# Delta rule: both directions of a chunk through the inverse in one tile, and the chunk's front joined likewise

## The chip, the cores and the metric

The kernel runs on 1 core of one Trainium2 chip. The metric is the device time of one execution in microseconds (us). TensorE multiplies matrices, VectorE, ScalarE and GpSimd work on tiles in SBUF (VectorE and ScalarE also read TensorE's results from PSUM), SyncE (SP) issues most transfers.

## What is computed

One layer of a hybrid encoder for 1024 tokens of width 1024 with 16 meta tokens ahead. Half of the mixer is a gated delta rule with 4 heads of 128, run forward and backward over the sequence; the other half is attention with 8 query heads. Both are projected out together, and a squared-ReLU MLP follows. The delta rule, in chunks, is what the change touches:

```python
decay = exp(where(incl, gc[..., :, None] - gc[..., None, :], -inf))
kk = einsum('bnhik,bnhjk->bnhij', k, k)
a_low = where(strict, kk * decay * beta[..., :, None], 0.0)
rhs = concatenate([v * beta[..., None], k * (beta * exp(gc))[..., None]], axis=-1)
uw = lax.linalg.triangular_solve(a_low + eye(C), rhs, left_side=True, lower=True, unit_diagonal=True)
...
def step(S, xs):
    v_new = u_i - w_i @ S
    o_i = q_i @ S + qk_i @ v_new
    S = S * gl_i + k_i.T @ v_new
```

## The kernel before

The kernel uses chunks of 128 tokens, so 8 per direction, and replaces the triangular solve by an explicit inverse of the unit triangular matrix of each chunk, head and direction (lower for the forward direction "f", upper for the backward one "b"). It is one program in which about twenty Python generators ("streams") each write out their own work in small steps. `progress` (L1538) decides the order in which the steps are written: it holds a clock of matmul time by its own formula (L88), a step that yields is due again after the latency in `LAT` (L79; 1.5 us for the inverse), and of the streams that are due the first in `URGENCY` (L74) goes next. The inverse stands ahead of the projection GEMM in that list, so its steps go in between the GEMM's groups of matmuls. The order of execution can still differ from the order in which steps are written, as the framework that builds the program places each engine's instructions.

The order of the stages: projection GEMM (`gemm`, L667), with short convolutions and norms behind each piece; beside it, as soon as keys and gates are there, `front` (L955), `kq_stream` (L1001) and the inverse; then `chain_open` (L1036) and the chain over the chunks (`chain`, L1065), which runs beside attention; the output projection; the MLP.

- `consts` (L32) makes the constant matrices on the host; `cgroup` (L142) loads a group of them in pieces of 512 columns through two staging tiles, `kdf` and `kdb`, and casts each on VectorE (L150).
- `open_prep` (L746) loads two such groups, the second (`dmg`, L760) with 14 masks of 128 columns and two of 128 for the decay, 2048 columns in all, and fills the fixed columns of the PM tiles with `pm_rest` (L777) on GpSimd.
- `front(c)`: the products of the keys (kk), the decays of both directions (exp on ScalarE, L970), their product dn (L972), the unit diagonal put in on GpSimd (L809), which gives the fp16 high part ah, and the low part al on VectorE (L978). Then the scaled keys kd (L988) and their store. It waits for the inverse and kq of chunk c - 2.
- `invert` (L820) for one direction of one chunk with 4 heads, in 15 steps. A first step transposes ah into X and masks X and Y (L833, L834). Then six levels of two steps: 4 matmuls of 64 columns into one PSUM tile and a mask on VectorE into pm (L844); 8 matmuls into one PSUM tile and two copies on ScalarE, into X and Y (L854, L855), with `pm_rest` on GpSimd. Then a correction step (9 matmuls, L865) and the result tt (4 matmuls, L870).
- Four streams run it, `inv00`, `inv10`, `inv01` and `inv11` (direction, parity of the chunk). The last one first inverts the meta tokens' matrix (`meta_inverse`, L895), with one head and three levels.
- `kq_stream`: products of keys and queries times the decay (L1016), stored.
- PSUM: psa has 3 tiles of 512 columns that the inverse, front and kq share (`psr`, L115); psg has 5 for the GEMM.
- `q_stream` (L1182) opens attention after the GEMM and the chain's opening.

Of the kernel before, what the change touches and what calls it, by code (L numbers as in the profile page):

```python
# [73 lines left out]
URGENCY = ("consts", "meta", "inv00", "inv10", "inv01", "inv11", "front", "kq", "chn", "chain0", "chain1", "wout", "wload",  # L74
# [7 lines left out]
def body(tc, I, out, dbg=None):  # L82
# [397 lines left out]
    def gates():  # L480
        for e in range(8):
            S.dma_start(ba[e * NM:(e + 1) * NM, :, 64:65], msscr[:, 0:16].rearrange("p (s e) -> p s e", s=2)[:, :, e:e + 1])
        tmp_g = keep("Df", 512)
# [262 lines left out]
    def open_prep():  # L746
# [4 lines left out]
        def stage():  # L751
            turn.append(0)
            return keep("kd" + "fb"[len(turn) % 2], 512)
# [6 lines left out]
        dmg = cgroup("f1", "ngt", F16, np_, stage)  # L760
# [7 lines left out]
        R.update(mk=mk, blk=blk, dm={(s, b): dmg(f"{s}{b}") for s in "fb" for b in (1, 2, 4, 8, 16, 32, 64)}, id16=id16, out=[dmg("nlt"), dmg("ngt")])  # L768
        for side in ("f0", "b0", "f1", "b1"):
            for i in range(2):  # L770
                PM[side, i] = np_.tile([P, NH * P], F16, name=f"pm{side}{i}", bufs=1)
                pm_rest(PM[side, i], NH, 2 << i, side[0] != "b")
            yield
# [3 lines left out]
    def pm_rest(pm, nh, b, lower):  # L777

        G.tensor_scalar(cols(pm, b, not lower).rearrange("p (h n) c -> p h n c", h=nh), rep4(cols(idf, b, not lower), nh),
                        1.0, 1.0, ALU.mult, ALU.mult)  # L780

    def rep4(ap, nh):
        return ap.unsqueeze(1).broadcast_to([P, nh, ap.shape[1], ap.shape[2]])
# [36 lines left out]
    def invert(nh, ah, al, side, key, levels, tt):  # L820

        w = nh * P
        lower = side == "f"
        other = "b" if lower else "f"
        dm, id16 = R["dm"], R["id16"]
        xy = keep("xy" + key, 2 * NH * P, F16)
        X, Y = xy[:, :w], xy[:, w:2 * w]
        ps = psr()  # L830
        for h in range(nh):
            T.matmul(v3(ps)[:, h], lhsT=v3(ah)[:, h], rhs=id16, start=True, stop=True)
        V.tensor_tensor(v3(X), v3(ps[:, :w]), rep(dm[side, 1], nh), ALU.mult)  # L833
        V.tensor_tensor(v3(Y), v3(ah), rep(dm[other, 1], nh), ALU.mult)  # L834
        yield
        for i, b in enumerate(levels):
            pm = PM[key, i % 2][:, :w]
            nb = 64 // b
            ps = psr()
            pv = ps[:, :w // 2].rearrange("p (h n c) -> p h n c", h=nh, c=b)  # L840
            for h in range(nh):
                T.matmul(pv[:, h], lhsT=v3(ah)[:, h], rhs=cols(v3(X)[:, h], b, lower), start=True, stop=True)
            mask = cols(dm[side, b], b, lower)
            V.tensor_tensor(cols(pm, b, lower).rearrange("p (h n) c -> p h n c", h=nh), pv,  # L844
                            rep4(mask, nh), ALU.mult)
            yield
            ps = psr()
            px = ps[:, :w // 2].rearrange("p (h n c) -> p h n c", h=nh, c=b)
            py = ps[:, w // 2:w].rearrange("p (h n c) -> p h n c", h=nh, c=b)
            for h in range(nh):  # L850
                T.matmul(px[:, h], lhsT=v3(Y)[:, h], rhs=cols(v3(pm)[:, h], b, lower), start=True, stop=True)
            for h in range(nh):
                T.matmul(py[:, h], lhsT=v3(pm)[:, h], rhs=cols(v3(Y)[:, h], b, not lower), start=True, stop=True)
            A.copy(cols(X, b, lower), px.rearrange("p h n c -> p (h n) c"))  # L854
            A.copy(cols(Y, b, not lower), py.rearrange("p h n c -> p (h n) c"))  # L855
            if i + 2 < len(levels) or i % 2:
                pm_rest(pm, nh, levels[i + 2] if i + 2 < len(levels) else levels[1], lower)
            yield
        ps = psr()
        T.matmul(v3(ps[:, :w]), lhsT=id16, rhs=rep(id16, nh), start=True, stop=False)  # L860
        for h in range(nh):
            T.matmul(v3(ps)[:, h], lhsT=v3(ah)[:, h], rhs=v3(X)[:, h], start=False, stop=False)
            T.matmul(v3(ps)[:, h], lhsT=v3(al)[:, h], rhs=v3(X)[:, h], start=False, stop=h == nh - 1)
        gt = PM[key, 0][:, :w]
        V.tensor_tensor(gt, ps[:, :w], X, ALU.subtract)  # L865
        yield
        ps = psr()
        for h in range(nh):
            T.matmul(v3(ps)[:, h], lhsT=v3(gt)[:, h], rhs=v3(Y)[:, h], start=True, stop=True)
        V.tensor_tensor(tt, ps[:, :w], Y, ALU.add)  # L870
        pm_rest(gt, nh, levels[0], lower)
# [11 lines left out]
    def consts_stream():  # L883
        yield from need("x")
        yield from open_prep()
        pl = keep("kdf", 512)
# [8 lines left out]
    def meta_inverse():  # L895
# [26 lines left out]
        yield from invert(1, ah, al, "f", "f1", (2, 4, 8), dn)  # L922
# [32 lines left out]
    def front(c):  # L955

        if c > 1:
            yield from need(f"inv0{c - 2}", f"inv1{c - 2}", f"kq{c - 2}")
# [3 lines left out]
        D, dn = {}, {}  # L962
        for d, side in FB:
            dn[d], D[d] = keep("dn" + side, 512), keep(f"D{side}{c % 2}", 512)
# [22 lines left out]
        for d, side in FB:  # L987
            V.tensor_tensor(v3(keep("kd" + side, 512)), v3(kT), bc(Erem[:, d, c], P), ALU.mult)  # L988
        yield
        for d, side in FB:  # L990
            S.dma_start(kscr[d * NT + c], keep("kd" + side, 512))
# [9 lines left out]
    def kq_stream():  # L1001

        yield from need("minv", *(f"q{h}" for h in range(NH)))
        for c in range(NT):
            yield from need(f"front{c}")
            D = {d: keep(f"D{side}{c % 2}", 512) for d, side in FB}
            qc = keep("qc", 512)
            S.dma_start(v3(qc), qscr[:, :, c * P:(c + 1) * P].rearrange("h p t -> p h t"))
            for d, side in FB:
                unit_diagonal(D[d], D[d])  # L1010
# [4 lines left out]
            for d, side in FB:  # L1015
                V.tensor_tensor(D[d], kq, D[d], ALU.mult)  # L1016
            yield
            for d, side in FB:
                S.dma_start(dscr[d * NT + c], D[d])
# [3 lines left out]
    def inv_stream(d, p):  # L1023

        side, key = "fb"[d], f"{'fb'[d]}{p}"
        if key == "f1":
            yield from meta_inverse()
        for c in range(p, NT, 2):
            yield from need(f"front{c}")
            tt = keep("tt" + side, 512)  # L1030
            yield from invert(NH, keep("ah" + key, 512, F16), keep("al" + key, 512, F16), side, key, (2, 4, 8, 16, 32, 64), tt)
            S.dma_start(tscr[d * NT + c], tt)
            mark(f"inv{d}{c}")


    def chain_open():  # L1036
        yield from need(*(f"inv{d}{c}" for d in range(2) for c in (NT - 2, NT - 1)), "meta", "kq")
# [519 lines left out]
    streams = dict(consts=consts_stream(), meta=meta_stream(), **{f"inv{d}{p}": inv_stream(d, p) for p in range(2) for d in range(2)},  # L1557
# [333 lines left out]
```

## Time and profile before

| | us |
|---|---|
| median of 3 runs (lowest to highest) | 1415.5 (1413.3 to 1420.03) |
| profiled execution | 1416.07 |
| its span | 1414.2 |
| TensorE busy | 1342.7 (95%) |
| VectorE busy | 1029.3 (73%) |
| ScalarE busy | 835.5 (59%) |
| GpSimd busy | 295.4 (21%) |

A profile is one execution of the program. Its page gives busy times of the engines, the windows view the same for a stretch of time with the granted clock of TensorE (1.00 is 2.4 GHz), the waits view the idle times of an engine by what ended them, the lines view groups of instructions with their mean duration, the tile view the same for one tile with first and last start, and the timeline the instructions one after another. A busy TensorE is one with a matmul in flight, and as matmuls overlap, the pace shows in the starts and not in the busy time.

### The profile page before, as it was taken

Reading aid. Unit: us, or ns where it says so; the run is one execution under the profiler, and the core shown is the slowest. Engines: PE = TensorE matmul, PEld = TensorE weight load, DVE = VectorE, ACT = ScalarE, POOL = GpSimd, SP = SyncE. Lnnn points to the kernel's source line nnn. Section 1 sums busy time; section 2 is a strip of 40 time slices with the busy share of each in tenths; the row PEclk is TensorE's granted clock in tenths of the full one; section 3 lists DMA queues with packets and bytes.
Section 4 is the critical chain, followed back from the end, with each engine's and each line's share of the span. In section 5 each row is a group of like instructions: output and inputs, shape, how many; then the busy total and the mean of one; then the engine's idle time right before and its main releaser. Section 6 shows DMA issues by size and latency. Waiting matters only on the chain. (4 is left out here: it accounts for less than half of the span.)

```text
span 1414.2 us, 26476 instructions
## 1 busy us (share of the span) xinstructions
PE 1342.7 (95%) x9627; PEld 1027.1 (73%) x9627; DVE 1029.3 (73%) x1962; ACT 835.5 (59%) x1747; POOL 295.4 (21%) x386
## 2 busy tenths in 40 slices
PE   6999999999998998899998799999999999999996
PEld 6999888777998877677777444444444888888875
DVE  5636779788768979877765987777775588675675
ACT  6556565756546777866644676666665455445552
POOL 1210234343534456533321200000000000000000
PEclk9999999999998999889999799999999999999998
DMA  6312234344379999997994354444443984466341
GB/s 209 87 57 62 83 98 158 112 149 153 121 253 282 245 264 239 221 242 186 224 225 135 102 175 158 153 155 150 158 155 114 331 271 127 142 193 194 98 150 66
DMA packets 273355, 236.86 MB, mean 167 GB/s; under 512 B 147484, under 2 KB 201656, under 8 KB 273224
## 3 DMA queue, kind: packets, MB, share of 16 engines
q1 hardware_dynamic: 270056, 225.73, 55.3%
q10 hardware_dynamic: 3168, 9.44, 1.8%
q8 instruction: 76, 1.25, 0.4%
q14 instruction: 55, 0.45, 0.1%
HBM read 132.27 MB, written 69.28 MB: 143 GB/s over the span
## 5 line engine op out<-in xcount | busy, mean ns | idle before, releaser
L95 PEld LDWEIGHTS <-wh 128*128 128x128 f16 x896 | 88.1, 99 | 102.7 <-issue 1.9
L95 PE MATMUL a<-woah 128*128 128x512 f32 x672 | 158.6, 390 | 1.3 <-DVE woah L1734 1.2
L95 PE MATMUL a<-woal 128*128 128x512 f32 x672 | 157.4, 389 | 0.0
L95 PEld LDWEIGHTS a<-woah 128*128 128x128 f32 x672 | 125.9, 188 | 29.0 <-DVE woah L1734 2.0
L95 PEld LDWEIGHTS a<-woal 128*128 128x128 f32 x672 | 126.1, 188 | 26.2
L95 PE MATMUL a<-uh,wh 128*128 128x344 f32 (+2 forms) x340 | 122.3, 360 | 0.7 <-ACT cw L665 0.5
L1270 POOL TENSOR_TENSOR P<-t,P 128x640 f16<-128x640 f32 x64 | 99.4, 1555 | 106.8 <-ACT P L1268 85.0
L95 PE MATMUL a<-ul,wh 128*128 128x344 f32 (+2 forms) x340 | 118.7, 349 | 0.5 <-DVE ul L262 0.5
L95 PE MATMUL a<-uh,wl 128*128 128x344 f32 (+2 forms) x340 | 118.3, 348 | 0.0
L161 POOL TENSOR_TENSOR rs<-ms,mhalf 128x1 f32<-128x1 f32 (+1 forms) x33 | 19.1, 578 | 424.0 <-DVE rs L1797 304.6
L1254 DVE TENSOR_REDUCE mx<-S 128x1 f32<-128x1024 f32 x64 | 77.9, 1219 | 24.3 <-PE S L95 24.1
L1262 ACT ACTIVATE t<-S,nb 128x1024 f32<-128x1024 f32 x64 | 71.5, 1117 | 40.8 <-DVE nb L1255 29.2
L95 PEld LDWEIGHTS <-pT 128*128 128x128 f16 x1536 | 59.5, 100 | 42.0 <-issue 26.6
L95 PE MATMUL o<-VP,pT 128*128 128x65 f16 (+1 forms) x1536 | 73.6, 198 | 11.3 <-DMA pT<-P 9.8
L95 PEld LDWEIGHTS <-wl 128*128 128x128 f16 x448 | 43.9, 98 | 54.1 <-issue 1.7
L1731 ACT ACTIVATE woah<-fr,isf 128x512 fp32r<-128x512 f32 x54 | 39.2, 725 | 70.3 <-PE a L95 61.0
L1731 ACT ACTIVATE woal<-fr,isf 128x512 fp32r<-128x512 f32 x54 | 39.2, 726 | 68.4 <-PE a L95 66.2
L1268 ACT CAST P<-t 128x1024 f16<-128x1024 f32 x64 | 66.8, 1043 | 4.7 <-DVE t L269 1.8
L1733 DVE SCALAR_TENSOR_TENSOR woah<-fr,isf,woah 128x512 fp32r<-128x512 f32 x54 | 40.5, 751 | 37.2 <-ACT woah L1731 37.1
L95 PE MATMUL S<-KH,qs 128*128 128x512 f32 x128 | 61.0, 476 | 6.5 <-ACT t L1262 6.5
L95 PEld LDWEIGHTS a<-uh,wh 128*128 128x128 f32 x340 | 65.0, 191 | 2.5 <-ACT cw L665 0.7
L95 PEld LDWEIGHTS a<-ul,wh 128*128 128x128 f32 x340 | 65.1, 192 | 2.1 <-DVE ul L262 1.0
(508 smaller groups left out, 3776.8 us busy)
## 6 DMA issues: line engine op xcount, KB each, us to landing
fr<-fscr SPq DMA_DIRECT2D x108, 256.0 KB
fscr<-os SPq DMA_DIRECT2D x64, 256.0 KB
rb<-in_w_down SPq DMA_DIRECT2D x64, 256.0 KB
fscr<-of SPq DMA_DIRECT2D x48, 256.0 KB
wr<-in_w_in SPq DMA_DIRECT2D x44, 256.0 KB
AQ<-in_w_up SPq DMA_DIRECT2D x22, 512.0 KB
raw<-in_w_up SPq DMA_DIRECT2D x10, 512.0 KB
X<-in_x SPq DMA_DIRECT2D x8, 512.0 KB
```

Of the source, the lines that this page charges most:

```text
L95: nc.tensor.matmul(out, lhsT=lhsT, rhs=rhs, **kw)
L161: G.tensor_tensor(dst, ms[:r, :n], mhalf[:r, :n], ALU.pow)
L1254: V.tensor_reduce(mx, s, AX.X, ALU.min)
L1262: A.activation(p32[:, :L], s, AF.Exp, bias=nb, scale=-1.0)
L1268: A.copy(p16[:, 0], p32[:, :L])
L1270: G.tensor_tensor(p16[:, 1, :LH], p32[:, :LH], p16[:, 0, :LH], ALU.subtract)
L1731: A.activation(ah, fr, AF.Copy, scale=isf[:, p:p + 1])
L1733: V.scalar_tensor_tensor(al, fr, isf[:, p:p + 1], ah.bitcast(F32), ALU.mult, ALU.subtract)
```

## The change

The two directions of a chunk share one tile of 1024 columns (ah, al, dn, D, kd, tt, X, Y, PM), a direction in each half. One stream per parity, `inv0` and `inv1`, takes both through the inverse. In a level the first step issues the 8 matmuls of both directions into one PSUM tile and masks all of it with one VectorE instruction of 512 columns; the second issues 16 into two PSUM tiles, one for X and one for Y, and copies each with one ScalarE instruction of 512 columns. The views `both` reach the cleared columns of one half and the other columns of the other half in one pattern, for which X, Y and PM are 128 columns wider. The masks are laid out at full width for this, so that the constants' second group grows from 2048 to 3584 columns; both staging halves lie in one tile kd. In the front, the diagonal (L809), al, kd and the kq product are one instruction for both directions. `pm_rest` still issues one instruction for each direction. The first step's transpose and mask of X, the correction and the result keep one instruction per direction. The meta tokens' inverse gets a function of its own with the steps it had.

```diff
     for b in (1, 2, 4, 8, 16, 32, 64):
-        m = (r // (2 * b) == c // (2 * b)) & ((r // b) % 2 == 1) & ((c // b) % 2 == 0)
-        parts[f"f{b}"] = m | (r == c)
-    for b in (1, 2, 4, 8, 16, 32, 64):
-        m = (r // (2 * b) == c // (2 * b)) & ((r // b) % 2 == 1) & ((c // b) % 2 == 0)
-        parts[f"b{b}"] = (m | (r == c)).T
+        m = ((r // (2 * b) == c // (2 * b)) & ((r // b) % 2 == 1) & ((c // b) % 2 == 0)) | (r == c)
+        clear = (np.arange(P) // b) % 2 == 0
+        parts[f"m{b}"] = np.concatenate([m, m.T] if b == 1 else [m[:, clear]] * NH + [m.T[:, ~clear]] * NH, axis=1)
...
-            return keep("kd" + "fb"[len(turn) % 2], 512)
+            return halves(keep("kd", 1024))[len(turn) % 2]
...
+    def halves(t):
+        return t[:, :512], t[:, 512:1024]
+
+    def pm_rest(pm, b, only=(0, 1)):
+
+        for s_, half in enumerate(halves(pm)):
+            if s_ in only:
+                G.tensor_scalar(cols(half, b, s_).rearrange("p (h n) c -> p h n c", h=NH), rep4(cols(idf, b, s_), NH),
+                                1.0, 1.0, ALU.mult, ALU.mult)
+
+    def both(t, b):
+
+        return t[:, :2 * (512 + b)].rearrange("p (s w) -> p s w", s=2)[:, :, :512].rearrange("p s (n t c) -> p s n t c", t=2, c=b)[:, :, :, 0]
...
-        G.affine_select(out=v3(dst), in_=v3(src), compare_op=ALU.not_equal, fill=1.0, base=0, pattern=[[0, NH], [1, P]], channel_multiplier=-1)
+        G.affine_select(out=v3(dst), in_=v3(src), compare_op=ALU.not_equal, fill=1.0, base=0, pattern=[[0, 2 * NH], [1, P]], channel_multiplier=-1)
...
-    def invert(nh, ah, al, side, key, levels, tt):
+    def invert(ah, al, p, tt):
...
+        levels = (2, 4, 8, 16, 32, 64)
         for i, b in enumerate(levels):
...
             ps = psr()
+            for d in range(2):
+                for h in range(NH):
+                    T.matmul(part(ps, d)[:, h], lhsT=v3(as_[d])[:, h], rhs=cols(v3(xs_[d])[:, h], b, not d), start=True, stop=True)
+            V.tensor_tensor(both(pm, b), wide(ps), wide(dm[b]), ALU.mult)
+            yield
+            px, py = psr(), psr()
+            for d in range(2):
+                for h in range(NH):
+                    T.matmul(part(px, d)[:, h], lhsT=v3(ys_[d])[:, h], rhs=cols(v3(ms_[d])[:, h], b, not d), start=True, stop=True)
+            for d in range(2):
+                for h in range(NH):
+                    T.matmul(part(py, 1 - d)[:, h], lhsT=v3(ms_[d])[:, h], rhs=cols(v3(ys_[d])[:, h], b, d), start=True, stop=True)
+            if i + 2 < len(levels) or i % 2:
+                pm_rest(pm, levels[i + 2] if i + 2 < len(levels) else levels[1])
+            A.copy(both(X, b), wide(px))
+            A.copy(both(Y, b), wide(py))
+            yield
...
-        for d, side in FB:
-            unit_diagonal(keep(f"ah{side}{c % 2}", 512, F16), dn[d])
-        yield
-        for d, side in FB:
-            V.tensor_tensor(keep(f"al{side}{c % 2}", 512, F16), dn[d], keep(f"ah{side}{c % 2}", 512, F16), ALU.subtract)
+        ah = keep(f"ah{c % 2}", 1024, F16)
+        unit_diagonal(ah, keep("dn", 1024))
+        yield
+        V.tensor_tensor(keep(f"al{c % 2}", 1024, F16), keep("dn", 1024), ah, ALU.subtract)
...
-        for d, side in FB:
-            V.tensor_tensor(v3(keep("kd" + side, 512)), v3(kT), bc(Erem[:, d, c], P), ALU.mult)
+        kd = keep("kd", 1024)
+        V.tensor_tensor(kd.rearrange("p (d h c) -> p d h c", d=2, h=NH), v3(kT).unsqueeze(1).broadcast_to([P, 2, NH, P]),
+                        Erem[:, :, c].unsqueeze(3).broadcast_to([P, 2, NH, P]), ALU.mult)
...
-            for d, side in FB:
-                V.tensor_tensor(D[d], kq, D[d], ALU.mult)
+            V.tensor_tensor(D.rearrange("p (d w) -> p d w", d=2), rep(kq, 2), D.rearrange("p (d w) -> p d w", d=2), ALU.mult)
...
-            yield from invert(NH, keep("ah" + key, 512, F16), keep("al" + key, 512, F16), side, key, (2, 4, 8, 16, 32, 64), tt)
-            S.dma_start(tscr[d * NT + c], tt)
-            mark(f"inv{d}{c}")
+            yield from invert(keep(f"ah{p}", 1024, F16), keep(f"al{p}", 1024, F16), p, tt)
+            for d in range(2):
+                S.dma_start(tscr[d * NT + c], halves(tt)[d])
+            mark(f"inv{c}")
```

## Rows read from the trace of the kernel before

**Rows 1.** Page, busy us (share of the span) and instructions of each engine.

```profile
PE 1342.7 (95%) x9627; PEld 1027.1 (73%) x9627; DVE 1029.3 (73%) x1962; ACT 835.5 (59%) x1747; POOL 295.4 (21%) x386
```

**Rows 2.** Windows: stretch, length, busy us (instructions) by engine, granted clock, DMA share, GB/s.

```profile
150.00:400.00 250.00, 245.39 (x2573) 207.69 (x2572) 196.74 (x416) 148.11 (x438) 93.54 (x171) 1.00 0.39 129
...
400.00:450.00 50.00, 46.00 (x346) 44.24 (x346) 35.22 (x89) 25.43 (x76) 16.73 (x18) 0.93 0.84 283
```

**Rows 3.** Waits of TensorE, 150 to 400 us: total us, times, longest.

```profile
PE a L95 <- DVE dnb L972: 1.4, 1, 1.4
```

**Rows 4.** Timeline of TensorE: start us, length us, what.

```profile
250.22 0.28 PE L95 MATMUL a<-pmf,xyf 128*128 128x64 f16 x4
250.34 0.28 PE L95 MATMUL a<-xyf,pmf 128*128 128x64 f16 x4
250.46 0.40 PE L95 MATMUL a<-uh,wh 128*128 128x344 f32 x1
250.70 0.32 PE L95 MATMUL a<-ul,wh 128*128 128x344 f32 x1
250.86 0.32 PE L95 MATMUL a<-uh,wl 128*128 128x344 f32 x1
...
251.50 0.29 PE L95 MATMUL a<-pmb,xyb 128*128 128x64 f16 x4
```

**Rows 5.** Timeline of TensorE: first and last burst of the inverse.

```profile
152.99 0.23 PE L95 MATMUL a<-id,ahm 128*128 128x128 f16 x1
...
388.78 0.40 PE L95 MATMUL a<-xyb,pmb 128*128 128x128 f16 x4
```

**Rows 6.** Tile views: duration ns min/median/max, first and last start us.

```profile
L1032 SPq DMA_DIRECT2D tscr<-ttb x8: 319/320/531, 202.0 to 391.7; - x8
...
L95 PE MATMUL a<-st,KT x128: 270/275/377, 401.8 to 563.1; 128*128 128x128 f32 x128
...
L95 PE MATMUL a<-wh,ul x128: 276/280/366, 348.1 to 416.3; 128*128 128x256 f32 x128
...
L95 PE MATMUL S<-KH,qs x128: 388/478/776, 435.8 to 720.2; 128*128 128x512 f32 x128
```

**Rows 7.** Lines of VectorE, 150 to 400 us: busy us, mean ns, idle before.

```profile
L844 DVE TENSOR_TENSOR pmf<-a,c_f 128x256 f16<-128x256 f32 (+1 forms) x51 | 20.7, 405 | 12.6 <-PE a L95 7.4 <-issue 3.2 <-POOL pmb L779 1.8
L844 DVE TENSOR_TENSOR pmb<-a,c_f 128x256 f16<-128x256 f32 x48 | 20.1, 419 | 6.2 <-PE a L95 5.6
...
L978 DVE TENSOR_TENSOR alf<-dnf,ahf 128x512 f16<-128x512 f32 x8 | 6.5, 817 | 0.2 <-POOL ahf L809 0.2
...
L870 DVE TENSOR_TENSOR ttf<-a,xyf 128x512 f32<-128x512 f32 x8 | 5.5, 685 | 2.1 <-PE a L95 2.1
```

**Rows 8.** Tile view of KH: a subtraction of 1024 columns.

```profile
L1168 DVE TENSOR_TENSOR KL<-t,KH x2: 1224/1224/1225, 422.5 to 423.6; 128x1024 fp32r<-128x1024 f32 x2
```

**Rows 9.** Lines of ScalarE, 150 to 400 us.

```profile
L854 ACT CAST xyb<-a 128x256 f16<-128x256 f32 x48 | 19.2, 401 | 4.0 <-PE a L95 3.9
...
L404 ACT COPY t<-a 128x512 f32<-128x512 f32 x8 | 4.8, 614 | 0.8 <-PE a L99 0.8
```

**Rows 10.** Timeline of ScalarE: first and last of four copies in a row.

```profile
248.05 0.43 ACT L854 CAST xyf<-a 128x256 f16<-128x256 f32 x1
...
248.84 0.47 ACT L855 CAST xyb<-a 128x256 f16<-128x256 f32 x1
```

**Rows 11.** Timeline of VectorE: masks of the two directions.

```profile
250.38 0.43 DVE L844 TENSOR_TENSOR pmf<-a,c_f 128x256 f16<-128x256 f32 x1 [0.80 <-PE a L95]
250.72 0.41 DVE L844 TENSOR_TENSOR pmb<-a,c_f 128x256 f16<-128x256 f32 x1
```

**Rows 12.** Timeline of SP and VectorE: staged constants, and the weights' low parts.

```profile
48.70 0.35 SPq L149 DMA_DIRECT2D kdb<-in_cst  x1
...
51.87 0.35 SPq L149 DMA_DIRECT2D kdb<-in_cst  x1
...
64.49 1.33 DVE L243 TENSOR_TENSOR wl<-wr,wh 128x544 fp32r<-128x544 f32 x2
```

More of the change, by code (lines that the diff above doesn't have):

```diff
@@ L767, in open_prep @@
         R.update(idb=idb, neg=neg[:3])
-        R.update(mk=mk, blk=blk, dm={(s, b): dmg(f"{s}{b}") for s in "fb" for b in (1, 2, 4, 8, 16, 32, 64)}, id16=id16, out=[dmg("nlt"), dmg("ngt")])
-        for side in ("f0", "b0", "f1", "b1"):
+        R.update(mk=mk, blk=blk, dm={b: dmg(f"m{b}") for b in (1, 2, 4, 8, 16, 32, 64)}, id16=id16, out=[dmg("nlt"), dmg("ngt")])
+        for p in range(2):
             for i in range(2):
-                PM[side, i] = np_.tile([P, NH * P], F16, name=f"pm{side}{i}", bufs=1)
-                pm_rest(PM[side, i], NH, 2 << i, side[0] != "b")
+                PM[p, i] = np_.tile([P, 2 * NH * P + P], F16, name=f"pm{p}{i}", bufs=1)
+                pm_rest(PM[p, i], 2 << i)
             yield
     PM = {}
-    def pm_rest(pm, nh, b, lower):
-        G.tensor_scalar(cols(pm, b, not lower).rearrange("p (h n) c -> p h n c", h=nh), rep4(cols(idf, b, not lower), nh),
-                        1.0, 1.0, ALU.mult, ALU.mult)
+    def halves(t):
[7 more added lines that the diff above has]
+        return t[:, :2 * (512 + b)].rearrange("p (s w) -> p s w", s=2)[:, :, :512].rearrange("p s (n t c) -> p s n t c", t=2, c=b)[:, :, :, 0]
     def rep4(ap, nh):
@@ L818, in cols @@
         return ap.rearrange("p (n s c) -> p n s c", s=2, c=b)[:, :, 0 if clear else 1, :]
-    def invert(nh, ah, al, side, key, levels, tt):
-        w = nh * P
-        lower = side == "f"
-        other = "b" if lower else "f"
+    def invert(ah, al, p, tt):
         dm, id16 = R["dm"], R["id16"]
[L828 to L834, printed above, removed]
+        X, Y = keep(f"x{p}", 1024 + P, F16), keep(f"y{p}", 1024 + P, F16)
+        xs_, ys_ = halves(X), halves(Y)[::-1]
+        as_, ls_, ts_ = halves(ah)[::-1], halves(al)[::-1], halves(tt)
+        first = dm[1].rearrange("p (s c) -> p s c", s=2)
+        for d in range(2):
+            ps = psr()
+            for h in range(NH):
+                T.matmul(v3(ps)[:, h], lhsT=v3(as_[d])[:, h], rhs=id16, start=True, stop=True)
+            V.tensor_tensor(v3(xs_[d]), v3(ps), rep(first[:, d], NH), ALU.mult)
+        V.tensor_tensor(Y[:, :1024].rearrange("p (s h c) -> p s h c", s=2, h=NH), ah.rearrange("p (s h c) -> p s h c", s=2, h=NH),
+                        first.unsqueeze(2).broadcast_to([P, 2, NH, P]), ALU.mult)
@@ L835, in invert, with part, wide @@
         yield
+        levels = (2, 4, 8, 16, 32, 64)
         for i, b in enumerate(levels):
-            pm = PM[key, i % 2][:, :w]
-            nb = 64 // b
-            ps = psr()
[L840 to L845, printed above, removed]
+            pm = PM[p, i % 2]
+            ms_ = halves(pm)
+            def part(ps, d):
+                return ps[:, d * 256:(d + 1) * 256].rearrange("p (h n c) -> p h n c", h=NH, c=b)
+            def wide(ps):
+                return ps.rearrange("p (s n c) -> p s n c", s=2, c=b)
+            ps = psr()
+            for d in range(2):
[8 more added lines that the diff above has]
+            for d in range(2):
+                for h in range(NH):
+                    T.matmul(part(py, 1 - d)[:, h], lhsT=v3(ms_[d])[:, h], rhs=cols(v3(ys_[d])[:, h], b, d), start=True, stop=True)
[4 more added lines that the diff above has]
+            yield
@@ new lines, in invert @@
+        gs_ = halves(PM[p, 0])
+        for d in range(2):
+            ps = psr()
+            T.matmul(v3(ps), lhsT=id16, rhs=rep(id16, NH), start=True, stop=False)
+            for h in range(NH):
+                T.matmul(v3(ps)[:, h], lhsT=v3(as_[d])[:, h], rhs=v3(xs_[d])[:, h], start=False, stop=False)
+                T.matmul(v3(ps)[:, h], lhsT=v3(ls_[d])[:, h], rhs=v3(xs_[d])[:, h], start=False, stop=h == NH - 1)
+            V.tensor_tensor(gs_[d], ps, xs_[d], ALU.subtract)
+        yield
@@ new lines, in invert, with invert_meta, blocks @@
+        for d in range(2):
+            ps = psr()
+            for h in range(NH):
+                T.matmul(v3(ps)[:, h], lhsT=v3(gs_[d])[:, h], rhs=v3(ys_[d])[:, h], start=True, stop=True)
+            V.tensor_tensor(ts_[d], ps, ys_[d], ALU.add)
+        pm_rest(PM[p, 0], levels[0])
+    def invert_meta(ah, al, tt):
+        dm, id16 = R["dm"], R["id16"]
+        X, Y = keep("x1", 1024 + P, F16)[:, :P], keep("y1", 1024 + P, F16)[:, :P]
+        ps = psr()[:, :P]
+        T.matmul(ps, lhsT=ah, rhs=id16, start=True, stop=True)
+        V.tensor_tensor(X, ps, dm[1][:, :P], ALU.mult)
+        V.tensor_tensor(Y, ah, dm[1][:, P:], ALU.mult)
+        yield
+        for i, b in enumerate((2, 4, 8)):
+            pm = PM[1, i % 2][:, :P]
+            def blocks(ap):
+                return ap.rearrange("p (n c) -> p n c", c=b)
+            ps = psr()[:, :64]
+            T.matmul(blocks(ps), lhsT=ah, rhs=cols(X, b, True), start=True, stop=True)
+            V.tensor_tensor(cols(pm, b, True), blocks(ps), blocks(dm[b][:, :64]), ALU.mult)
@@ L846, in invert @@
             yield
             ps = psr()
[L848 to L854, printed above, removed]
@@ L855, in invert @@
-            A.copy(cols(Y, b, not lower), py.rearrange("p h n c -> p (h n) c"))
-            if i + 2 < len(levels) or i % 2:
-                pm_rest(pm, nh, levels[i + 2] if i + 2 < len(levels) else levels[1], lower)
-            yield
[L859 to L863, printed above, removed]
@@ L864, in invert @@
-        gt = PM[key, 0][:, :w]
-        V.tensor_tensor(gt, ps[:, :w], X, ALU.subtract)
-        yield
[L867 to L871, printed above, removed]
+            T.matmul(blocks(ps[:, :64]), lhsT=Y, rhs=cols(pm, b, True), start=True, stop=True)
+            T.matmul(blocks(ps[:, 64:P]), lhsT=pm, rhs=cols(Y, b, False), start=True, stop=True)
@@ new lines, in invert_meta @@
+            if i != 1:
+                pm_rest(PM[1, i % 2], 8 if i == 0 else 2, (0,))
+            A.copy(cols(X, b, True), blocks(ps[:, :64]))
+            A.copy(cols(Y, b, False), blocks(ps[:, 64:P]))
+            yield
+        ps = psr()[:, :P]
+        T.matmul(ps, lhsT=id16, rhs=id16, start=True, stop=False)
+        T.matmul(ps, lhsT=ah, rhs=X, start=False, stop=False)
+        T.matmul(ps, lhsT=al, rhs=X, start=False, stop=True)
+        gt = PM[1, 0][:, :P]
+        V.tensor_tensor(gt, ps, X, ALU.subtract)
@@ L873, in kcol @@
+        yield
+        ps = psr()[:, :P]
+        T.matmul(ps, lhsT=gt, rhs=Y, start=True, stop=True)
+        V.tensor_tensor(tt, ps, Y, ALU.add)
+        pm_rest(PM[1, 0], 2, (0,))
     def kcol(h, c):
@@ L921, in meta_inverse @@
         yield
[L922 removed]
+        yield from invert_meta(ah, al, dn)
         yield
@@ L1555, in progress @@
                 st.remove(s)
-    streams = dict(consts=consts_stream(), meta=meta_stream(), **{f"inv{d}{p}": inv_stream(d, p) for p in range(2) for d in range(2)},
+    streams = dict(consts=consts_stream(), meta=meta_stream(), inv0=inv_stream(0), inv1=inv_stream(1),
                    front=front_stream(), kq=kq_stream(), chn=chain_open(), chain0=chain_stream(0), chain1=chain_stream(1), wout=wout_stream(),
```

36 lines of the change are left out of this document (17 added, 19 removed).

## The prediction

> **What bounds the kernel now.** Read the page's busy shares first: TensorE is busy for 95% of the span [rows 1], so nothing that is shortened on another engine counts by itself; it counts only where TensorE waits for it or is made to do more. Next comes the place of the change. The inverse's matmuls start at 152.99 us and end at 388.78 us [rows 5], inside the projection GEMM, so the windows view of 150 to 400 us is the one to ask: TensorE is busy 245.39 of 250 us at a granted clock of 1.00, VectorE 196.74 us, ScalarE 148.11 us, GpSimd 93.54 us [rows 2]. Only 4.6 us of TensorE idle is left to win there, and the waits view splits it into small pieces: its longest entry is 1.4 us, before the kq matmul [rows 3].
>
> "Busy" hides one more cost, and the matmul timeline shows it. The inverse's fp16 matmuls of 64 columns come in bursts between the GEMM's fp32r matmuls of 344 columns; eight of them take 0.24 us (250.22 to 250.46), 0.03 each. After a burst the second fp32r matmul starts 0.24 us behind the first (250.46 to 250.70), where the third follows at the usual 0.16 us (250.86) [rows 4]. So every return from a burst costs some 0.08 us that counts as busy. Going through the timeline from the first burst to the last [rows 5] I count 167 bursts with matmuls of the inverse, with a median loss of 88 ns on return: 14.7 us of TensorE time in this stage. This is the only thing on the critical engine that the change can touch, since the number and the shapes of the matmuls stay as they are.
>
> Last, what follows: the inverse's last store is issued at 391.7 us, the chain's first matmul starts at 401.8 us, the last GEMM matmul at 416.3 us and the first attention score at 435.8 us [rows 6]. Attention waits for the GEMM and for the chain's opening (q_stream, L1183), and here the GEMM is the later one, by 416.3 - 401.8 = 14.5 us. An inverse that ends a little earlier therefore gains nothing by itself, and one that ends up to 14.5 us later doesn't hold attention back.
>
> **The change part by part.**
>
> *Matmuls and bursts.* Per chunk and direction: 4 + 6 x 12 + 9 + 4 = 89 matmuls, before and after; no gain, no loss from their number. Before, a step of one direction issues 4 or 8 of them and the four streams put 8 x 2 x 15 = 240 steps into 167 bursts, some joined, some split; in the rows the second direction's products came at 251.50, apart from the first's at 250.22, and so paid a return of its own [rows 4]. After, both directions are one step: 8 chunks x 15 = 120 steps. If each is its own burst there are 120; two streams that meet make fewer, and the 16-matmul step, which now takes two of the three PSUM tiles of psa, may be split and make more. I take 125: 42 fewer x 0.088 us = -3.7 us. Ends: none fewer (0), and 100 bursts, -5.9 us.
>
> *VectorE.* 96 masks of 256 columns (mean of 405 and 419 ns, 0.412 us) become 48 of 512; the 512-column op from PSUM takes 0.685 us [rows 7]: 39.6 - 32.9 = 6.7 us less. The 16 subtractions for al (up to 0.817 us [rows 7]) become 8 of 1024 columns; a subtraction of 1024 columns takes 1.22 us [rows 8]: at most 13.1 - 9.8 = 3.3 us less. The kd and kq products likewise, 16 of 0.685 to 8 of 1.22 each: 1.2 us less each. Together about 12 us of 196.74. VectorE is not the bound, so this is worth only what TensorE waits for: 0 taken, the whole 4.6 us of idle [rows 2] as the end below nothing, and the same amount as the end above, since a joined op also makes the first direction wait for the second.
>
> *ScalarE.* 192 copies of 256 columns (0.40 us) become 96 of 512 (0.614 us) [rows 9]: by durations 77 - 59 = 18 us less. But four copies in a row start at 248.05 and 248.84 us, so 0.26 us apart [rows 10]; by that spacing 192 cost 50 us and the gain is about nothing. I take nothing, as copies are off the bound either way. The Trainium skill (page "ScalarE: Activation LUTs", section "What ACT_TABLE_LOAD costs") says that back-to-back activations overlap by about 93 ns. This speaks against this half of the change: by that figure 192 copies already save 18 us of their durations (an estimate), all that joining them would save. The trace agrees and goes further, by 0.40 - 0.26 = 0.14 us; the sum is the same by either.
>
> *Latency of a step.* Joined, a step's result is there for both directions at once. Two masks started at 250.38 and 250.72 and the second ended at 251.13, 0.75 us after the first began; one of 512 columns takes 0.685 us [rows 7, 11]. Four copies end at 249.31, 1.26 us after the first began [rows 10]; two of 0.614 take 1.23 us. So the later direction loses nothing, and only the first loses its lead: at most 0.39 us per mask step (0.27 more of mask, 0.12 for four more matmuls) and 0.45 us per copy step (0.21 of copy, 0.24 for eight matmuls). In a chunk's seven of each that is 5.9 us, and with four chunks one behind the other in a stream 23 us. The two directions already march side by side, so I take 2 us of it, which lies within the 14.5 us of slack [rows 6] and costs 0. The planner's share is also small: a step's due time (LAT, L79) now counts from the end of both directions' matmuls, 0.107 to 0.213 us of its clock later. Ends: 0 and 23 us.
>
> *GpSimd.* pm_rest keeps two instructions per step; the diagonals go from 32 of 512 to 16 of 1024. GpSimd is busy 93.54 of 250 us [rows 2]; 0.
>
> *Constants.* The masks grow from 2048 to 3584 columns, so the staged group has 7 loads instead of 4, each waiting on SP for the cast two before it. Two such loads start 3.17 us apart (48.70 to 51.87); three more are 4.8 us at most, with three casts on VectorE, and behind them on SP stand the loads of the next projection's weights, two of whose low parts are made as late as 64.49 us [rows 12]. I take +0.5 us; ends 0 and +4.8. The masks themselves are needed from 153 us on, far behind.
>
> *DMA stores.* The same stores of 256 KB, but the first direction's waits for the second's result; they wait on SP before as well. 0.
>
> Sum: -3.7 + 0.5 = -3.2 us. The profiled execution took 1416.07 us (span 1414.2 and 1.9 around it), so 1412.9; the median of the three runs, 1415.5, is 0.6 lower, so **1412 us**. A measurement of this kernel tells about 0.5% (7 us) from no change, so this forecast counts as "same".
>
> **The rivals.**
>
> *More is freed (faster).* The joined streams meet in one burst more often (100 bursts, -5.9 us) and VectorE's 12 us take away all 4.6 us of idle: -10.5 us, 1405. For it: VectorE is busy 79% of the stage [rows 2], and 240 steps in 167 bursts means that steps come together already. Against it: the idle is made of many causes, and the longest is no wait of the inverse [rows 3].
>
> *The inverse's line gets too long (slower).* All the lost leads add up: 23 us, the chain opens at 401.8 + 23 = 424.8 us, 8.5 us behind the last GEMM matmul, and attention starts that much later: 1424. It decides from 14.5 us on, 0.26 us per step in 4 x 14 steps. For it: a step that takes two of three PSUM tiles makes the other stream, the front and kq wait for a tile. Against it: the later direction's result is no later than now [rows 10, 11]. In the 400 to 450 us window TensorE is already short of work (46.00 of 50 us, clock 0.93) [rows 2], so a delay there would not be made up.
>
> *Nothing joins.* The 16-matmul step is split at the second PSUM tile, or the directions were adjacent nearly everywhere already, the bursts stay at 160 or more, and what is left is the constants' 0.5 us: 1416.
>
> **How the numbers follow.** Forecast 0.45; nothing joins 0.15; more is freed 0.24; too long a line 0.16. Faster by over 0.5% (below 1408.4) has the 0.24, slower (above 1422.6) the 0.16, the rest 0.60. The range reaches to 1403 below, which leaves out about a tenth, and to 1423 above, which takes in the constants' end (1412 + 4.3 and the idle's +4.6) and most of the way to 1424.
>
> **What the changed profile would show.** Bursts of the inverse near 125 in place of 167, with the same 0.24 us at each return; 48 masks of about 0.69 us, and 96 copies of about 0.61; the last GEMM matmul near 413 us; the last store of the inverse between 387 and 396 us. The forecast is wrong if the GEMM's end moves by more than 6 us, if the first attention score no longer follows the last GEMM matmul by about 19.5 us, or if TensorE waits between 60 and 70 us for the weights. A shift that shows up only behind 436 us would come from the order of chain, attention and projection, which I have costed at nothing.

## The result, and the profile after

The changed kernel takes 1434.0 us (median; 1431.2 to 1435.9) where the kernel before takes 1414.7 beside it. The ratio of their runs is on record as 1.0124, 95% interval 1.0105 to 1.0143 (the two medians alone give 1.0136). I had forecast 1412 us and a range up to 1423. In the rows below L93 answers to L95 of before, L861 to L844, L872 and L873 to L854 and L855, L1086 to L1032, L1277 to L1223.

The page's first part and the windows of the inverse's stage and the one behind it (to be read beside [rows 1, 2]). The windows give busy us (instructions) of TensorE, its weight loads, VectorE, ScalarE and GpSimd, then the granted clock, DMA share and GB/s:

```profile
PE 1337.0 (93%) x9627; PEld 1028.2 (72%) x9627; DVE 1035.4 (72%) x1885; ACT 831.9 (58%) x1653; POOL 300.3 (21%) x370
```

```profile
150.00:400.00 250.00, 241.93 (x2574) 208.91 (x2574) 195.86 (x336) 145.12 (x343) 99.35 (x159) 1.00 0.38 126
400.00:450.00 50.00, 40.25 (x310) 38.84 (x309) 32.60 (x80) 24.88 (x76) 15.24 (x17) 0.90 0.81 275
```

TensorE does its work in 5.7 us less and still ends 19 us later, so the time went into waits. In the inverse's stage its busy time falls by 3.5 us, about what the bursts were to bring; behind 400 us it loses 5.75 us in the first 50 us alone. The tile views tell where the landmarks went ([rows 6] for before):

```profile
L1086 SPq DMA_DIRECT2D tscr<-tt x16: 319/320/403, 201.2 to 397.0; - x16
...
L93 PE MATMUL a<-st,KT x128: 270/275/560, 407.7 to 585.0; 128*128 128x128 f32 x128
...
L93 PE MATMUL a<-wh,ul x200: 276/282/366, 61.9 to 412.9; 128*128 128x256 f32 x64, 128*128 128x272 f32 x32, 128*16 128x272 f32 x4
...
L93 PE MATMUL S<-KH,qs x128: 387/476/776, 435.5 to 733.6; 128*128 128x512 f32 x128
...
L93 PE MATMUL a<-rr,at x128: 270/275/377, 418.3 to 602.8; 128*128 128x128 f32 x128
```

The inverse's last store is 5.3 us later (391.7 to 397.0) and the chain begins 5.9 us later (401.8 to 407.7). The GEMM ends 3.4 us earlier and the first score is where it was (435.8 and 435.5). But the chain's last matmul (the last row, a<-rr,at) is at 602.8, where before it was at 582.7, 20 us later. In this pair of traces nothing is made up behind it: 830.6 us pass from the chain's end to the span's end, 831.5 before. In the code the output projection does wait for the chain's end (`wout_stream`). The chain's end does not set the end by itself, though: over all the traces of this case that stretch is between 826.7 us (b_chn16) and 839.2 us (a_lat13).

The 20 us are not the 5.9 us grown larger. The chain's first step (both directions) ends at 420.3 us before and at 421.9 after, so most of the late opening is made up by then. The first new loss comes right behind it. TensorE's timeline, the kernel before and then the changed one:

```profile
421.12 2.05 PE L95 MATMUL a<-st,KT 128*128 128x128 f32 x16 [0.87 <-DVE st L1107]
425.19 2.89 PE L95 MATMUL a<-rr,tt 128*128 128x128 f32 x16 [2.02 <-DVE rr L1078]
427.74 1.95 PE L95 MATMUL a<-idr,t 128*128 128x128 f32 x8
```

```profile
420.72 1.16 PE L93 MATMUL a<-rr,at 128*128 128x128 f32 x8 [1.32 <-DVE st L1161]
429.63 1.97 PE L93 MATMUL a<-idr,t 128*128 128x128 f32 x8 [7.75 <-DVE t L1277]
431.39 3.46 PE L93 MATMUL a<-st,KT 128*128 128x128 f32 x16
```

Before, the chain's second step (a<-st,KT, then a<-rr,tt) fills the time until attention's first q tile (a<-idr,t) is there. After, the q tile is written ahead of the second step; TensorE stands 7.75 us before it, and the second step starts at 431.4, 10.3 us later than before. The q tile in its turn waits for the load of its rows, which GpSimd can use from 427.16 on:

```profile
427.16 1.04 POOL L1275 TENSOR_TENSOR AQ<-AQ,nsc 128x512 f32<-128x512 f32 x1 [10.05 <-DMA AQ<-aqscr]
```

The chain's second step has its input (st) from 423.4 us on. The Trainium skill (page "TensorE: Matmul & The Clock Gate", section "Step-by-step: what each phase is for") says that TensorE starts its matmuls in program order and that only weight loads run ahead. The trace agrees: in the 7.75 us before the q tile no matmul of the chain gets past the q tile.

Further on it is the products of attention that wait for the transposed probabilities (pT, brought by SP). TensorE's waits from 400 to 820 us, before and after:

```profile
PE o L95 <- DMA pT<-P: 9.8, 8, 2.4
```

```profile
PE o L93 <- DMA pT<-P: 22.0, 12, 5.6
PE a L93 <- DVE t L1277: 7.8, 1, 7.8
...
PE o L93 <- DVE t L1277: 4.2, 1, 4.2
```

In all, TensorE is idle for 42.4 us of these 420 before and for 60.4 after; the granted clock is 0.94 in both. The 18.0 us between them are the delay of the MLP's start (798.0 to 816.0).

### The profile page after: what moved, and what is told of

Read it like the earlier page. It is cut to its first block, busy times and chain, and to the rows that moved or that the text cites. A ratio compares the mean times of both kernels' runs of the same rounds, so it can differ in the third digit from the quotient of the medians.

```text
span 1433.4 us, 26179 instructions
## 1 busy us (share of the span) xinstructions
PE 1337.0 (93%) x9627; PEld 1028.2 (72%) x9627; DVE 1035.4 (72%) x1885; ACT 831.9 (58%) x1653; POOL 300.3 (21%) x370
## 5 line engine op out<-in xcount | busy, mean ns | idle before, releaser
L93 PEld LDWEIGHTS <-wh 128*128 128x128 f16 x896 | 88.0, 99 | 102.3 <-issue 1.3
L93 PE MATMUL a<-woah 128*128 128x512 f32 x672 | 158.2, 390 | 1.2 <-DVE woah L1788 1.2
L93 PE MATMUL a<-woal 128*128 128x512 f32 x672 | 157.4, 389 | 0.0
L93 PEld LDWEIGHTS a<-woah 128*128 128x128 f32 x672 | 126.0, 188 | 28.3 <-DVE woah L1788 2.0
L93 PEld LDWEIGHTS a<-woal 128*128 128x128 f32 x672 | 126.1, 188 | 26.2
L93 PE MATMUL a<-uh,wh 128*128 128x344 f32 (+2 forms) x340 | 121.4, 357 | 0.8 <-ACT cw L663 0.6
L93 PE MATMUL a<-ul,wh 128*128 128x344 f32 (+2 forms) x340 | 117.9, 347 | 0.8 <-DVE ul L260 0.8
L93 PE MATMUL a<-uh,wl 128*128 128x344 f32 (+2 forms) x340 | 116.9, 344 | 0.0
L93 PEld LDWEIGHTS <-pT 128*128 128x128 f16 x1536 | 58.8, 99 | 59.9 <-DMA pT<-P 31.1
L93 PE MATMUL o<-VP,pT 128*128 128x65 f16 (+1 forms) x1536 | 73.5, 197 | 28.8 <-DMA pT<-P 22.0
L93 PEld LDWEIGHTS <-wl 128*128 128x128 f16 x448 | 43.9, 98 | 54.0 <-issue 1.6
L782 POOL TENSOR_SCALAR pm<-c_id 128x256 f16<-128x256 f32 x107 | 58.3, 564 | 87.6 <-PE a L93 79.7
L93 PE MATMUL S<-KH,qs 128*128 128x512 f32 x128 | 61.4, 480 | 6.6 <-ACT t L1316 6.6
L93 PEld LDWEIGHTS a<-ul,wh 128*128 128x128 f32 x340 | 65.3, 192 | 3.0 <-DVE ul L260 1.4
L93 PEld LDWEIGHTS a<-uh,wh 128*128 128x128 f32 x340 | 65.1, 191 | 2.8 <-ACT cw L663 0.7
```

The costliest lines, as they stand in the source:

```text
L93: nc.tensor.matmul(out, lhsT=lhsT, rhs=rhs, **kw)
L782: G.tensor_scalar(cols(half, b, s_).rearrange("p (h n) c -> p h n c", h=NH), rep4(cols(idf, b, s_), NH), 1.0, 1.0, ALU.mult, ALU.mult)
```

## The experiments

**Theories.** *Order*: the joined steps end later on the planner's clock, so the chain is opened later, and the written order of chain, q tiles and products on TensorE changes for the worse. *Path*: the joined inverse is slower on the chip, and the later opening costs by itself, us for us or more. The planner's clock is worked out when the program is written and is no time of the chip. On it the last inverse ends at 306.6 before and at 311.7 after, and the chain's first step is due `CH_` behind the chain's opening step: at 317.7 before, 322.85 after. (These times come from writing the program out and reading its clock.)

**The delay alone, and the change without it.** Two kernels swap the two orders:

```diff
 b_chn11, in the kernel before
-TS_, TP_, CH_, Q0_ = 2.55, 13.8, 6.0, 6.42
+TS_, TP_, CH_, Q0_ = 2.55, 13.8, 11.0, 6.42
 a_chn1, in the changed kernel
-TS_, TP_, CH_, Q0_ = 2.55, 13.8, 6.0, 6.42
+TS_, TP_, CH_, Q0_ = 2.55, 13.8, 1.0, 6.42
```

> The kernel before, with one number changed: the chain's opening is marked 5 us later on the planner's own clock (CH_ 11 instead of 6); nothing of the inverse is joined. Order theory (the changed kernel is slower because its chain opens later against attention's opening, so that on TensorE the first q tile stands ahead of the chain's second step): about 1433 us, 1426 to 1438, with a TensorE wait of 5 to 8 us for the q tile's low part near 422 us. Rival (the joined tiles and instructions themselves slow the later stages, by their place in memory or their transfers): 1415 us, within 4.

> The changed kernel, with the chain's opening marked 5 us earlier on the planner's clock (CH_ 1 instead of 6); the inverse stays joined and ends as late as in the changed kernel. Order theory: 1411 us (1407 to 1416), the 3.4 us by which the GEMM ends earlier being kept at most, and the wait for the q tile's low part below 2 us. Rival (the joined work itself): 1430 to 1436.

b_chn11, in which nothing is joined: 1433.2 us, ratio 1.0115 (1.0095 to 1.0136), within the intervals the whole loss. Its waits are those of the changed kernel:

```profile
PE o L95 <- DMA pT<-P: 22.3, 10, 4.9
PE a L95 <- DVE t L1223: 7.2, 1, 7.2
PE o L95 <- DVE t L1223: 4.1, 1, 4.1
```

a_chn1, in which all is joined: 1417.4 us, ratio 1.0009 (0.9991 to 1.0027). Its inverse is as late as that of the changed kernel (last product 395.0, against 394.8 there and 389.0 before), yet the chain runs from 402.3 to 581.9 as before. Behind the opening its planner's clock is that of the kernel before (the GEMM's end at 336.3, the chains' ends at 475.6 and 476.5 in both), so the swap gives back the whole written order there. So the loss is the order's, and the joined inverse by itself is worth nothing that shows, between -0.1% and +0.3%. The two also part what I would have read as one: the GEMM's end at 413 is there in b_chn11 as well (413.0), so it is the order's doing; with the order of before the joining moves it from 416.3 to 415.0 only.

**Is it the one long wait?** a_q12 writes the q tile later in the changed kernel (`Q0_` 6.42 to 12.0), a_lat13 makes the inverse's steps due earlier (`inv` in `LAT` 1.5 to 1.3).

> The changed kernel, with the first q tile due 5.6 us later on the planner's clock (Q0_ 12 instead of 6.42), so that the chain's second step goes ahead of it; the chain opens as late as in the changed kernel. Order theory: the wait of 7.75 us near 422 us goes, and the chain ends at least as much earlier: 1418 to 1427. If only the chain's later start counts and not the order: 1430 to 1436.

> The changed kernel, with a step of the inverse due 1.3 us after the one before it instead of 1.5. Order theory: the inverse ends some 9 us earlier on the planner's clock, earlier than in the kernel before, the chain opens before 402 us, and the time is 1404 to 1415. Rival (a step's result comes too late for its successor since a step is joined, so that TensorE waits for the masks): the waits for the masks grow from 4.3 us to 10 or more and the time stays above 1428.

Both missed what was expected of them. a_q12: 1433.5 us (1.0129, 1.0098 to 1.0161), though the chain's second step starts at 423.9 and the waits for pT are 11.6 us. TensorE still waits 5.8 us for q tiles, in three pieces, and attention's last score is at 729.8 (720.4 before). So the one 7.75 us wait is not the cause by itself. a_lat13: 1433.0 us (1.0116, 1.0093 to 1.0139). On the planner's clock the inverse does end 9 us earlier (302.8), which puts the chain's due time at 313.9, 3.8 us earlier than in the kernel before. On the chip TensorE then stands idle for 11.3 us of the inverse's stage (8.1 in the changed kernel), the chain opens at 405.4, the GEMM ends at 427.7 and the first score comes at 445.1, 9.3 us later than before. So a_lat13 doesn't test the late opening alone: its order is one with an earlier chain, to be read beside the earlier opening below, and its idle time is another loss on top.

**How the loss goes with the shift.** The kernel before with `CH_` 3.5, 8.5 and 16.0, beside 6.0 and 11.0:

> The kernel before with the chain's opening 2.5 us later on the planner's clock (CH_ 6.0 to 8.5; nothing joined). With 5 us more (CH_ 11) the time had risen by 16 us. Theory 'line': each us of delay costs about 3 us, so this gives some +8 us, 1423 to 1427. Theory 'fit': the written order of before happens to fit, and any other order of the chain, the q tiles and the scores loses about the same; then this gives +12 to +20 us, 1429 to 1437, or, if the order hardly moves with 2.5 us, the time of before, 1413 to 1420.

> The kernel before with the chain's opening 10 us later on the planner's clock (CH_ 6.0 to 16.0; nothing joined). Theory 'line' (3 us for each us of delay): +30 us, 1440 to 1450. Theory 'fit' (another order loses some 16 us, whatever the size of the shift): 1427 to 1437; plus at most the 5 us by which the opening is later still than with CH_ 11, 1442.

> The kernel before with the chain's opening 2.5 us earlier on the planner's clock (CH_ 6.0 to 3.5; nothing joined). Theory 'fit' (the order of before is one that fits, and its neighbours lose): slower than before, 1422 to 1434. Theory 'late' (what comes later is worse, what comes earlier is as good or better): 1410 to 1418.

| opening, us of the planner's clock | -2.5 | 0 | +2.5 | +5 | +10 |
|---|---|---|---|---|---|
| ratio to before | 1.0079 (1.0052 to 1.0106) | 1 | 1.0089 (1.0072 to 1.0106) | 1.0115 (1.0095 to 1.0136) | 1.0095 (1.0075 to 1.0116) |
| chain, first to last matmul | 399.0 to 593.8 | 401.8 to 582.7 | 405.2 to 595.6 | 407.8 to 601.0 | 411.0 to 599.4 |
| GEMM's last matmul | 420.9 | 416.3 | 415.0 | 413.0 | 410.9 |
| attention's last score | 743.1 | 720.4 | 728.7 | 730.7 | 719.6 |

No line: 2.5 us in either direction cost 11 to 13 us, and 10 us cost no more than 5. An opening that is earlier on the chip, at 399.0, loses as well, which a theory that only a later opening costs doesn't allow. Two lines have to be fed out of one queue. Written earlier, the chain's steps stand among the GEMM's, the GEMM ends 4.6 us later, attention falls behind by 23 us and the chain by 11; written later, the chain falls behind by 13 to 18. The order of before stands between.

**What in the inverse's stage took the bursts' gain back?** In a_chn1 TensorE waits there for the joined mask:

```profile
PE a L93 <- DVE pm L861: 4.4, 5, 1.9
```

GpSimd's and VectorE's timeline at the longest of the five, the one that ends at 359.78 (rows of the other engines left out):

```profile
354.89 2.82 POOL L565 TENSOR_TENSOR t<-t,t 16x128 f32<-16x128 f32 x2
354.98 3.01 DVE L728 TENSOR_TENSOR bst<-bst,qt 128x256 f32<-128x256 f32 x1
...
357.92 1.21 DVE L1043 TENSOR_TENSOR kd<-a,dec 128x1024 f32<-128x1024 f32 x1
359.05 1.27 DVE L861 TENSOR_TENSOR pm<-a,c_m 128x512 f16<-128x512 f32 x2
```

The mask starts at 359.05, behind 4.2 us of other work on VectorE. Most of that is one instruction: bst takes 3.01 us, where the median of its 16 is 0.42, while GpSimd is at work on t<-t,t. a_c1_mask takes a_chn1 and splits the joined mask, a_c1_front splits the front's joined VectorE instructions instead:

```diff
 a_c1_mask
-            V.tensor_tensor(both(pm, b), wide(ps), wide(dm[b]), ALU.mult)
+            for s in range(2):
+                V.tensor_tensor(both(pm, b)[:, s], wide(ps)[:, s], wide(dm[b])[:, s], ALU.mult)
 a_c1_front (al and kd likewise)
-            V.tensor_tensor(D.rearrange("p (d w) -> p d w", d=2), rep(kq, 2), D.rearrange("p (d w) -> p d w", d=2), ALU.mult)
+            for D_ in halves(D):
+                V.tensor_tensor(D_, kq, D_, ALU.mult)
```

> The changed kernel with CH_ 1.0 (the order behind the opening as before: 1417.4 us, GEMM's last matmul 415.0, TensorE waits 4.4 us for pm in 150 to 400 us), and the joined mask issued as one instruction for each direction. If the mask's length is what TensorE waits for, as each direction waits for both: the 4.4 us fall to under 2 us and the GEMM ends at 412.5 to 413.5. If the mask starts late, because VectorE has other work in front of it (bst of 3.01 us, kd of 1.21 us): a first half of 0.41 us in place of 0.68 saves 0.27 us on each of 5 waits, so 3 us of the 4.4 stay and the GEMM ends at 414 to 415. The total within 3 us of 1417 either way.

> The changed kernel with CH_ 1.0 and the front's joined VectorE instructions (al, kd and the kq product, 1024 columns, 1.2 us each) issued as one of 512 columns for each direction; the inverse stays joined. If the long instructions of the front are what the masks wait behind: the 4.4 us of waits for pm fall to 2 to 3 us. If not (two halves of 0.68 us stand in front of the mask just as one of 1.21 did): 4 to 5 us. The total within 3 us of 1417 either way.

The waits fall to 2.9 us with the mask split and to 3.3 with the front split:

```profile
PE a L93 <- DVE pm L862: 2.9, 4, 1.9
```

```profile
PE a L93 <- DVE pm L861: 3.3, 3, 2.0
```

Both totals lie near what a late start predicts, but they are made of other waits than in a_chn1. The wait at 359.8 is gone in both kernels: there bst takes 0.41 us and no longer coincides with GpSimd's t<-t,t. The longest is now one that was 1.1 us in a_chn1 (at 287.8), where the mask starts behind eight short instructions of the front (dn, 2.15 us together). In a_c1_mask and in a_c1_front:

```profile
289.40 0.28 PE L93 MATMUL a<-pm,y 128*128 128x64 f16 x4 [1.92 <-DVE pm L862]
```

```profile
290.16 0.40 PE L93 MATMUL a<-pm,y 128*128 128x64 f16 x8 [1.95 <-DVE pm L861]
```

So the totals don't decide between the mask's length and its late start. Two waits that have the same neighbours with the mask whole and split say more: 0.31 and 0.19 us (near 239 us), 0.41 and 0.48 us (near 325 us). There the mask's length is worth 0.1 us at most, and what it starts behind is other work of VectorE. What the front's split is worth is not shown. Neither is a gain: bursts with the inverse go from 124 to 133 in a_c1_mask (123 in a_c1_front), and the GEMM ends at 416.5 and 416.8, later than either theory had it for a_c1_mask; the times are 1420.2 (1.0015, 1.0002 to 1.0028) and 1419.7 us (1.0016, 0.9999 to 1.0034). The profiled execution of a_c1_front has a span of 1426.4 us, well above its median, so nothing behind this stage is read from it.

**Are the transposes the loss?** SP is 2.5 us (median) in the issue of each of the 64 transposes. Five kernels halve them, which brings TensorE's waits for them down to between 1.6 and 6.3 us, and read the high half twice:

```diff
-        S.dma_start_transpose(pT, p16.rearrange("p a b -> p (a b)"))
+        S.dma_start_transpose(pT[:, :8], p16[:, 0])
...
-            term(ob[:, j * W:(j + 1) * W], pT[:, k], pT[:, 8 + k], VP[:, k, kv], j == 0 and k == 0, False)
+            term(ob[:, j * W:(j + 1) * W], pT[:, k], pT[:, k], VP[:, k, kv], j == 0 and k == 0, False)
```

> The kernel before; the transposing transfer of each attention head (64 of them, SP is 2.7 us in each, 173 us in all) moves only the high half of P, and the products that read the low half read the high one (so the attention's low part is left out; TensorE's work is unchanged). Theory 'order on TensorE alone': 1410 to 1418, as TensorE waits only 9.8 us for these transfers. Theory 'transfers': down by the 5 to 10 us of those waits, 1405 to 1412.

> The changed kernel with the same halved transposing transfers. Its distance to the kernel before with them is what counts; with whole transfers it is 16 to 19 us. Theory 'transfers' (the later opening loses because the transposes on SP's queue come late for the order that is written): the distance falls to under 6 us. Theory 'order on TensorE alone' (TensorE waits in its order for work of ScalarE, VectorE and GpSimd, whatever SP does): it stays at 12 to 19 us.

> The changed kernel with attention's first q tile written later (Q0_ 6.42 to 12.0, which takes away the single wait of 7.7 us for it) and with halved transposing transfers (the attention's low part left out, as in b_half). Beside b_half, 1407.1, and a_half, 1420.6. Theory 'two waits' (the q tile's wait and the waits for the transposes are what the other order costs): 1407 to 1413. Theory 'many waits' (the loss is spread, and what is taken from one place comes back in another): 1416 to 1422.

> The kernel before with the opening 2.5 us earlier (CH_ 3.5: 1430.4, where TensorE waits 21 us for transposes in 400 to 820 us in place of 9.8) and halved transposing transfers. Theory 'two waits': the loss goes with the transposes' waits, 1407 to 1412. Theory 'many waits': 1416 to 1422, 10 to 14 us above b_half.

> The kernel before with the opening 2.5 us later (CH_ 8.5: 1429.6, waits for transposes 19.6 us) and halved transposing transfers. Theory 'two waits': 1407 to 1412. Theory 'many waits': 1416 to 1422.

| order | whole transposes, us above before | halved, us above b_half (1407.1) |
|---|---|---|
| changed kernel | 19.3 | 13.6 (1420.6) |
| changed, q tile later | 16.2 | 12.0 (1419.1) |
| before, opening -2.5 | 13.1 | 12.4 (1419.5) |
| before, opening +2.5 | 11.8 | 2.8 (1409.8) |

For an opening of 2.5 us later the loss is the transposes': 9 of 11.8 us go with them. For the others most of it is not; with the waits for pT at 2.6 to 6.3 us, 12 to 14 us stay. In a_half the 7.6 us wait for the q tile is still there and the chain's second step is 12.7 us behind that of b_half (433.4 and 420.7); in b_chn3_half the GEMM ends 6.7 us later than in b_half (422.6 and 415.9) and the first score comes 6.2 us later. Which pair of instructions costs what in each of these orders stays open. What is shown is that no one wait makes the loss in all of them.

## Why the prediction was wrong, step by step

- *Bursts: right.* 124 with matmuls of the inverse where I took 125 and before had 167 [rows 5], with a median loss of 85 ns on return (86 by the same count in before); TensorE's busy time in the stage fell by 3.5 us (forecast 3.7).
- *VectorE's relief, worth 0: wrong by 3.5 us.* My bounds for it were the whole idle of 4.6 us on either side, and the end above came. Masks shrank as said (40.8 to 33.4 us, forecast -6.7), kd and kq by 1.2 us each as said. al grew by 1.0 us (12.3 to 13.3) where I had up to 3.3 less. Half of its eight take the 1.21 us that I had read off KL; the other half take 2.1 us, each with GpSimd at work beside it (but so has one of the short ones, all along). In all VectorE's busy time in the stage fell by 0.9 us (196.74 to 195.86) and not by about 12. For ScalarE I had counted by the spacing of starts, for VectorE by durations, though its masks had overlapped too (0.34 us apart at 0.42 each [rows 11]). The idle of TensorE in the stage went from 4.6 to 8.1 us, with 4.3 us of waits for the mask, where before the longest entry of any kind was 1.4 us [rows 3]. These waits begin behind other work on VectorE. That the other direction, when it was a step of its own, would have filled them is argued and not shown. The bursts' 3.5 us were paid back within the stage: the GEMM's matmul number 1541 of 1620, counted through the timeline, starts at 401.7 us before and at 401.9 after.
- *ScalarE: right.* 96 copies of 0.589 and 0.599 us in place of 192 of 0.40; busy in the stage falls by 3.0 us only, where the durations would give 20. The copies had overlapped before, as [rows 10] showed.
- *Constants: right.* By the same count GEMM matmul number 402 starts 0.4 us later (95.3 to 95.7); forecast 0.5.
- *Latency of a step: the size was off, and the price.* I took 2 us and had 23 as the end; it was 5.3 at the inverse's last store and 5.1 on the planner's clock. I called the planner's share small, 0.107 to 0.213 us for a step. Over the 60 steps of a stream's four chunks that is 6 to 13 us where nothing else sets the due time, and that clock holds nothing but matmul times and due times, so the 5.1 us are what the joined steps add there.
- *"Lies within the 14.5 us of slack and costs 0": the step that failed.* The slack was attention's alone, and attention's start did hold (435.5 us; 22.6 behind the GEMM's end, not 19.5). But the inverse also opens the chain, and on the planner's clock the chain's place in the order moved with it, by 5.1 us. That shift alone costs 15.9 us in b_chn11, of the changed kernel's 19.3. I had read that the GEMM is the later of two conditions of q_stream and forgot the stream that has only the other. It is not that the results came too late on the chip: in a_chn1 the inverse's last store is as late (397.2) and the chain starts 5 us behind it, at 402.3, where before 10 us lay between them [rows 6].
- *The order, costed at nothing: 12 to 19 us.* I named it as where a shift behind 436 us would come from. b_chn11 shows that the order makes the loss without any joining, and b_chn3 that an earlier opening loses as well.
- *The GEMM's end: luck.* It came at 412.9, with "near 413" forecast. The forecast was of fewer bursts; b_chn11, with none joined, has 413.0, and a_chn1, with all joined, 415.0.
- *The rivals.* "Too long a line" had the right beginning and the wrong point from which it decides: it needed 14.5 us of delay and 23 for 1424, where 5.3 were enough for 1434. "Nothing joins" gives the right time for the joining alone (a_chn1, 1417.4 against 1416) for a wrong reason: the bursts did join.

## What to carry to other kernels

Where a program's order is written out by a planner and run by engines that keep it, a change that moves a due time is two changes: test the shift alone in the old kernel and the new work with the shift undone before either is judged. Slack has to be read for every stream that the moved work releases, not for the one that is nearest. And a saving on the bound engine's own overhead counts only if the joined work doesn't make that engine wait elsewhere: here 3.5 us saved came back as 3.5 us of idle time in the same stage.

## What the runs showed of the hardware that I had not expected

The transposes on SP's queue hold the kernel before itself: the issue of one takes 2.5 us (median; 172.8 us summed over the 64), and of half a one 1.2 us. With them halved (and attention's low half left out) the kernel takes 1407.1 us, 0.9925 (0.9908 to 0.9942) of before. That is 10 us, while the waits that name the transposes fell by 5.5 us only, from 9.8 to 4.3. The issue time and the bytes were halved together, so the runs don't tell which of the two counts. Whole, and then halved:

```profile
L1274 SPq DMA_TRANSPOSE pT<-P x64: 1577/2545/6613, 449.1 to 730.1; - x64
```

```profile
L1274 SPq DMA_TRANSPOSE pT<-P x64: 1231/1238/3988, 444.4 to 720.3; - x64
```

So between 450 and 730 us TensorE is not the only bound, and a kernel that issues fewer or shorter transposes there would have something to win, which joining the inverse's directions has not.

And an instruction of VectorE took seven times its usual time beside one of GpSimd: bst took 2.97 to 3.02 us in five traces (the changed kernel, a_chn1, a_q12, a_half and a_q12_half), each time with GpSimd's t<-t,t beside it for nearly all of that time, and 0.41 us at the same place in a_c1_mask, where the two don't meet. What holds it is not tested here.
